# One streaming encoder layer on one core: the recurrence's two-operand GpSimd work goes to VectorE, and one PSUM bank goes from the projections to the recurrence

## The chip, the cores and the metric

The kernel runs on one core of a Trainium2 chip. The metric is the device time of one execution in microseconds, as the median of several runs. Every product is computed in float32 precision: a float32 operand is split into a high part (rounded to the matmul's input format) and a low part (the rest), and three matmuls (high x high, high x low, low x high) stand for one. So TensorE does three times the plain work, and each operand needs a cast on ScalarE and a subtraction on another engine.

## The reference

One layer of a hybrid encoder, 1024 prompt rows and 128 rows of running streams, model width 1024:

```
h = rms_norm(x); p = h @ w_in            # columns: RWKV r,k,v,loras | FoX q,k,v,forget | merge gates
u = p_r + (shifted(p_r) - p_r) * mu      # width-2 token shift
S_t = S_{t-1} * w_t + (S_{t-1} a_t) b_t + v_t k_t ;  y_t = S_t r_t     # 8 heads, 64 x 64 state
o_a = (groupnorm(y) + bonus) * g         # g = sigmoid(gate lora) @ g2: "the gate's product"
o_b = softmax(q k^T / 8 + c_t - c_s) v   # forgetting attention, 8 heads
x = x + (sig(g_a) * (o_a @ p_a) + sig(g_b) * (o_b @ p_b)) @ w_out
x = x + (silu(n @ w_gate) * (n @ w_up)) @ w_down ,  n = rms_norm(x);   y = rms_norm(x)
```

The decay w_t, a_t, b_t and k_t come from small lora products; kk, the normalised key, needs the sum of squares of a head's keys ("key sums").

## The kernel before, in words

The rows are normalised and transposed first. Then 14 column tiles of the RWKV projections run (`rwkv_tile`), and after them a long stretch in which TensorE alternates between the recurrence and more projections.

**The queue of projections.** `gemm_fm` cuts each projection tile (128 columns by 3 groups of 384 rows) into 8 pieces of 3 matmuls per group; the pieces stand in one list, `fq`. `D(n)` takes n pieces from it, `W(us)` takes as many as fill so many microseconds at 0.52 us each. Each group of rows of a tile accumulates in one PSUM bank of the pool `psg` (tag gm); the bank is free again when ScalarE and VectorE have read it (`evac`). The k and v tiles of the attention are transposed besides: a function `later`, put in `pending`, is run by `flush` behind the last matmul of the next tile, and its three transposes (L916) write a bank of the same pool. The weights of a tile are loaded one tile ahead (`w_in_tile`), cast by ScalarE (L146) and their low part subtracted (L147), on GpSimd for these tiles.

**The recurrence** (`rwkv_unit`) runs over 6 units of 192 rows (3 chunks of 64), all 8 heads at once. Per unit: products of the scaled keys and queries ("gram", L588), which are masked (`masked`, L581); the inverse of a triangular matrix, by a loop of 30 small VectorE operations (L617, L619) and products (L652 to L689); then three chunks in turn, each with a chain TensorE, VectorE, TensorE, VectorE and ScalarE, TensorE (L725, `solve_u`, L737, L748). The next unit's `prologue` (loras L438, key sums L447, bonus L497) and the previous unit's `epilogue` (mean L506, variance L512, gate's product L524) are generators that `step(nxt)` and `step(last)` move on by one stage, at written places in the unit. They, the gram, the transposes and the inverse take their PSUM banks from the pool `psr`, tag ms. Three more banks of `psr` hold the outputs y0, y1 and the chunk's products.

**The order.** In this stretch TensorE's order is the order in which the code is written (`manual_schedule`). The other engines' queues are ordered by a scheduler that goes by its own clock; `hi` asks it to put a step ahead, and instructions recorded through `hi` have the line of that helper, L388 in the kernel before (389 in the changed one). An engine works through its queue strictly in order.

Behind the recurrence come the attention of the prompt, one head after another, with the remaining projections between (`fox_d`), the streams' attention and the merge, the output product and the feed-forward part, which take the second half of the time.

Of the kernel before, what the change touches and what calls it, by code (L numbers as in the profile page):

```python
# [17 lines left out]
P = 128  # L18
# [35 lines left out]
def hybrid_kernel(ctx: ExitStack, tc: tile.TileContext, d, o):  # L54
# [110 lines left out]
    h_lo = [hp.tile([P, NK, G], F32R, name=f"hl{g}") for g in range(NG)]  # L165
    psg = pool("psg", 3, PSUM, side="right", stack=sth)
    stg = pool("stg", 2, side="right", stack=sth)
# [8 lines left out]

    def parameters(pl):
        prow = pl.tile([46, P], F32, name="prow", bufs=1)
# [9 lines left out]
        dma(sh_in, d["state_shift"][0, :, 0, :].rearrange("b (c p) -> (b c) p", p=P))  # L188
        pps = psg.tile([P, 512], F32, tag="gm", name="pps")
# [4 lines left out]
        shps = psg.tile([P, 512], F32, tag="gm", name="shps")  # L194
        T.transpose(shps[:, :14 * NB], sh_in, ident[:14 * NB, :14 * NB])
# [16 lines left out]
    def w_in_tile(c0, M):  # L212
        return load_w(wp1, d["w_in"][0, :, c0:c0 + M].rearrange("(k p) m -> p k m", p=P), NK, M, f"c{c0}", eng=GP)

# [73 lines left out]
    first += [rwkv_tile(ct) for ct in (4, 5)]  # L288
    with tc.tile_pool(name="ph0", bufs=3, reuse_waits="tile", side="left") as ph0:
        g1B = None  # L290
        for i in range(NTT):
            xt = ph0.tile([P, DM], F32, tag="xt", name="xt", bufs=6)
            dma(xt, xrow(i))
            if i == 0:
                g1B = row_gain(ph0, d["norm1_g"], "g1B")
            if i == 3:
                parameters(ph0)
            hn = ph0.tile([P, DM], F32, tag="hn", name="hn")
            norm_T(xt, hn, g1B, i, h_hi, h_lo, psg, "gm")
            if i % 3 == 2:  # L300
                for t_ in first:
                    fq += t_[NK * (i // 3):NK * (i // 3 + 1)]
            D(first_d[i])
        D(len(fq) - first_left)
        first.clear()
# [49 lines left out]
    def ms():  # L355
        return psr.tile([P, 512], F32, tag="ms", name="ms")

# [170 lines left out]
    def rwkv_unit(u_, us, nu, pre, last):  # L528
# [14 lines left out]
        V.tensor_tensor(BK[:, :, 2, :], ch3(k2), ch3(e3), op=mult)  # L543
        GP.tensor_tensor(BK[HS[1], :, 0, :], ch3(k2)[HS[1]], ch3(e3)[HS[1]], op=mult)

# [6 lines left out]
        for hd in range(2):  # L552
            GP.tensor_tensor(TT[HS[hd], :, hd, 1, :], ch3(ur)[HS[hd]], ch3(e2)[HS[hd]], op=mult)
        SV = [ch3(tt_()) for _ in range(2)]
# [17 lines left out]

        def masked(dst, src, c0, hs, eng=V):
            n0 = 0
            late_ = [final and (c0 + n) % NC3 >= 1 for n in range(4)]
            while n0 < 4:
                n1 = n0 + 1
                while n1 < 4 and late_[n1] == late_[n0]:
                    n1 += 1
                mk = (gmask_s if late_[n0] else gmask)[hs].unsqueeze(1).broadcast_to([hs.stop - hs.start, n1 - n0, 2, C])  # L580
                eng.tensor_tensor(dst[:, n0:n1], src[hs, n0:n1], mk, op=mult)  # L581
                n0 = n1

        for c0 in range(0, NC12, 4):
            pg = [psr.tile([P, 4, 2, C], F32, tag="ms", name="gram") for _ in range(2)]
            for c in range(4):
                for hd in range(2):
                    T.matmul(pg[hd][:, c], both(hd, c0 + c), TT[HS[hd], c0 + c, hd], start=True, stop=True)  # L588
            for hd in range(2):
                masked(GB[HS[hd], c0:c0 + 4], pg[hd], c0, HS[hd])  # L590
                S.copy(TT[OP[hd], c0:c0 + 4, hd], pg[hd][OP[hd]])
            W(2.1)
        step(last)
        for hd in range(2):
            for c0 in range(0, NC12, 4):
                masked(TT[OP[hd], c0:c0 + 4, hd], TT[:, c0:c0 + 4, hd], c0, OP[hd], GP)
        gab, grb = GB[:, :, 0, :], GB[:, :, 1, :]
# [7 lines left out]
        goff = tt_()[:, 0:NC12 * 32].rearrange("p (c t) -> p c t", t=32)  # L605
        GP.tensor_tensor(goff, dg[:, 0:NC12, :], low16.unsqueeze(1).broadcast_to([P, NC12, 32]), op=mult)
        L = inv_tile()
# [25 lines left out]
        V.transpose(XL[:, 0:32, :], X[:, 0:32, :])  # L633
        step(nxt)
        step(last)
        W(2.6)
        step(nxt)
        W(2.1)
        step(nxt)
        W(2.1)  # L640
        step(nxt)
        step(last)
        W(4.2)
        xd = XL[:, 0:32, 0:NC12].rearrange("p t c -> p c t")
# [75 lines left out]
        for c in range(ncp):  # L720
# [6 lines left out]
            for hd, hs in enumerate(HS):  # L727
                hi(GP.tensor_tensor, sts[hs], SV4[hd][hs, :, c, :], sc[hs, :, c:c + 1].broadcast_to([64, 4, 64]), op=mult)
            for y in range(4):
# [31 lines left out]
        def streams(z):  # L761
# [16 lines left out]
            for cc in range(2):  # L778
# [16 lines left out]
                for y in range(2):  # L795
                    i = (y0 + y) * NC3 + c
                    uvm = tt_()[:, 0:512].rearrange("p (h b t) -> p h b t", h=2, b=4)
                    Z = psr.tile([P, 512], F32, tag="ms", name="zs")[:, 0:256]
                    for hd, hs in enumerate(HS):
# [460 lines left out]
    def merge(g):  # L1260
        w, cur = [], []

        def piece(ct, q):
            if ct == 0 and q == 0:
                branch_b(g)
            if ct % 2 == 0 and q == 0:
# [4 lines left out]
                S.copy(hi, raw)  # L1271
                GP.tensor_tensor(lo, raw, hi.bitcast(F32), op=sub)
                w[:] = [hi, lo]
# [434 lines left out]
```

## Time and profile before

| | |
|---|---|
| runs | 2143.20, 2152.05, 2159.08 us; median 2152.05 |
| profiled execution | 2142.85 us, span 2141.1 us, granted clock 0.965 |
| busy, share of span | PE 1983.0 us (93%), VectorE 1213.8 (57%), ScalarE 822.5 (38%), GpSimd 358.7 (17%) |
| projections up to the recurrence | about 60 to 200 us: PE 140.0 of 140.0 us busy |
| recurrence, units 0 and 1 | 200 to 432 us: PE 205.2 us busy, clock 0.92 |
| recurrence, units 2 to 5 | 432 to 756 us: PE 298.9 us busy, clock 0.97 |
| streams of the recurrence, head 0 | 756 to 864 us: PE 94.3 us busy, clock 0.95 |

PE is TensorE, DVE VectorE, ACT ScalarE, POOL GpSimd. [...] A profile row is one of a stage table, a wait, a group of instructions, or one instruction in time; the times are us from the start of the span.

### The profile page before, as it was taken

How to read it: one execution, taken by the hardware profiler on the slowest of the kernel's cores; microseconds unless marked ns; L12 is line 12 of the kernel's file. 1: busy time of each engine (PE TensorE's matmuls, PEld its weight loads, DVE VectorE, ACT ScalarE, POOL GpSimd, SP SyncE). 2: the span in 40 equal slices, each digit the busy share in tenths (PEclk: the TensorE clock that was granted, in tenths of full speed). 3: DMA queues.
4: the chain of work that ended last, by engine and by line, in shares of the span. 5: the costliest groups of instructions: out<-in, count | busy, mean ns of one | idle time of the engine just before them, and what ended most of it. 6: DMA issues, size and time to landing. Idle time of an engine off the chain costs nothing. (4 is left out here: it accounts for less than half of the span.)

```text
span 2141.1 us, 38241 instructions
## 1 busy us (share of the span) xinstructions
PE 1983.0 (93%) x15472; PEld 1798.3 (84%) x15472; DVE 1213.8 (57%) x2274; ACT 822.5 (38%) x1569; POOL 358.7 (17%) x401
## 2 busy tenths in 40 slices
PE   7999988889898998879989898699999999999998
PEld 7998877778787977767868797699999999888887
DVE  5112576655756644668746524866666666564445
ACT  5323445362644433557644213522333223221113
POOL 3322423234243411010033103000000000000004
PEclk9999999899999999989999999799999999999999
DMA  5332333212221224676467517322312222452212
GB/s 168 108 92 87 106 91 95 66 57 73 64 62 49 81 73 107 175 208 178 129 209 249 160 58 247 97 78 71 95 62 73 71 67 89 143 208 84 84 63 89
DMA packets 234997, 233.66 MB, mean 109 GB/s; under 512 B 41678, under 2 KB 209252, under 8 KB 234820
## 3 DMA queue, kind: packets, MB, share of 16 engines
q1 hardware_dynamic: 163012, 159.85, 25.4%
q10 hardware_dynamic: 71280, 69.26, 9.7%
q8 instruction: 122, 2.00, 0.4%
q0 software_dynamic: 528, 2.10, 0.3%
q14 instruction: 55, 0.45, 0.1%
HBM read 157.53 MB, written 73.70 MB: 108 GB/s over the span
## 5 line engine op out<-in xcount | busy, mean ns | idle before, releaser
L152 PE MATMUL gm<-hh,hi_c 128*128 128x384 f32 (+1 forms) x1032 | 375.4, 364 | 1.5 <-DVE vl L928 0.7
L154 PE MATMUL gm<-hh,lo_c 128*128 128x384 f32 (+1 forms) x1032 | 353.0, 342 | 1.6 <-POOL lo_c L147 1.6
L153 PE MATMUL gm<-hl,hi_c 128*128 128x384 f32 (+1 forms) x1032 | 353.4, 342 | 0.3 <-DVE hl L136 0.3
L152 PEld LDWEIGHTS gm<-hh,hi_c 128*128 128x128 f32 (+1 forms) x1032 | 197.3, 191 | 17.6 <-issue 3.1
L153 PEld LDWEIGHTS gm<-hl,hi_c 128*128 128x128 f32 (+1 forms) x1032 | 197.4, 191 | 4.8 <-issue 0.8
L154 PEld LDWEIGHTS gm<-hh,lo_c 128*128 128x128 f32 (+1 forms) x1032 | 196.8, 191 | 4.4 <-POOL lo_c L147 2.2
L1619 PE MATMUL dn<-hi_d,ah 128*128 128x512 f32 x396 | 155.5, 393 | 4.0 <-ACT ah L1437 4.0
L1620 PE MATMUL dn<-lo_d,ah 128*128 128x512 f32 x396 | 155.0, 391 | 0.0
L1621 PE MATMUL dn<-hi_d,al 128*128 128x512 f32 x396 | 154.0, 391 | 0.0
L1639 POOL TENSOR_TENSOR yo<-x,gF 128x512 f32<-128x512 f32 x17 | 21.9, 1288 | 783.1 <-DVE x L1623 773.4
L147 POOL TENSOR_TENSOR lo_c<-raw_c,hi_c 128x1024 fp32r<-128x1024 f32 (+1 forms) x43 | 103.2, 2401 | 242.5 <-ACT hi_c L146 228.7
L1623 DVE TENSOR_TENSOR x<-x,dn 128x512 f32<-128x512 f32 x108 | 73.6, 686 | 114.5 <-PE dn L1621 113.7
L266 DVE SCALAR_TENSOR_TENSOR su<-gm,omu,sh 128x384 f32<-128x384 f32 (+1 forms) x42 | 24.1, 573 | 122.7 <-ACT sh L262 95.9
L1619 PEld LDWEIGHTS dn<-hi_d,ah 128*128 128x128 f32 x396 | 74.9, 189 | 20.5 <-ACT ah L1437 4.9
L1621 PEld LDWEIGHTS dn<-hi_d,al 128*128 128x128 f32 x396 | 74.9, 189 | 16.2 <-DVE al L1438 0.5
L1620 PEld LDWEIGHTS dn<-lo_d,ah 128*128 128x128 f32 x396 | 74.9, 189 | 15.5
L1437 ACT CAST ah<-raw_act 128x1152 fp32r<-128x1152 f32 x22 | 25.5, 1158 | 156.3 <-PE dn L1620 136.7
L1405 PE MATMUL po<-hi_o,mh 128*128 128x256 f32 x288 | 81.8, 285 | 4.0 <-ACT hi_o L146 4.0
L1406 PE MATMUL po<-lo_o,mh 128*128 128x256 f32 x288 | 82.0, 285 | 0.5 <-DVE lo_o L147 0.5
L1407 PE MATMUL po<-hi_o,ml 128*128 128x256 f32 x288 | 81.8, 284 | 0.0
L146 ACT CAST hi_c<-raw_c 128x1024 fp32r<-128x1024 f32 (+1 forms) x43 | 44.3, 1029 | 72.8 <-PE gm L153 62.0
L1508 PE MATMUL m<-t2h,s2h 128*128 128x256 f32 (+1 forms) x176 | 53.5, 304 | 12.3 <-ACT t2h L1437 12.3
(495 smaller groups left out, 5396.6 us busy)
## 6 DMA issues: line engine op xcount, KB each, us to landing
raw_c<-in_w_in SPq DMA_DIRECT2D x42, 512.0 KB
raw_act<-a_s SPq DMA_DIRECT2D x22, 576.0 KB
raw_w_gate<-in_w_gate SPq DMA_DIRECT2D x22, 512.0 KB
raw_w_up<-in_w_up SPq DMA_DIRECT2D x22, 512.0 KB
raw_d<-in_w_down SPq DMA_DIRECT2D x22, 512.0 KB
g_s<-sg ACTq DMA_DIRECT2D x48, 192.0 KB
u_s<-su ACTq DMA_DIRECT2D x42, 192.0 KB
a_s<-act ACTq DMA_DIRECT2D x22, 320.0 KB
```

The costliest lines, as they stand in the source:

```text
L147: eng.tensor_tensor(lo[:, :, c0:c0 + M], raw, hi[:, :, c0:c0 + M].bitcast(F32), op=sub)
L152: T.matmul(ps, wh(k), xh(k), start=(k == 0), stop=False)
L153: T.matmul(ps, wh(k), xl(k), start=False, stop=False)
L154: r = T.matmul(ps, wl(k), xh(k), start=False, stop=(k == nk - 1))
L1405: T.matmul(ps[:, :Q], mh, hi[:, k, :], start=(k == 0), stop=False)
L1406: T.matmul(ps[:, :Q], mh, lo[:, k, :], start=False, stop=False)
L1407: T.matmul(ps[:, :Q], ml, hi[:, k, :], start=False, stop=(k == NK - 1))
L1508: T.matmul(ps, ah[:, k, :], bh[:, k, :], start=(k == 0), stop=False)
L1619: T.matmul(ps, ah[:, ts_], wh[:, cs], start=(x == 0), stop=False)
L1620: T.matmul(ps, ah[:, ts_], wl[:, cs], start=False, stop=False)
L1621: T.matmul(ps, al[:, ts_], wh[:, cs], start=False, stop=(x == n - 1))
L1623: r = V.tensor_tensor(xs, xs, ps, op=add)
```

## The change

All two-operand GpSimd instructions of the recurrence and of the weights that run beside it become VectorE instructions: the low parts of the projection weights (L147) and of p_b (L1272), the key product BK (L544), two scalings TT (L553), the scaled state `sts`, the off-diagonal part `goff` (L606). The second half of the gram, which ScalarE copied out of PSUM (L591) and GpSimd then masked (L581), is masked by VectorE straight from PSUM; the ScalarE copy goes. The pool of the recurrence gets three banks for ms, that of the projections two; the normalisation before has its own four banks, freed before the recurrence begins. In the unit, the third stage of `last` (gate's product) stands ahead of the stage of `nxt` that has the key sums, its second stage gets a filler behind the first of `nxt`, and the fillers there are 26 pieces a unit, 24 before.

```diff
-    psg = pool("psg", 3, PSUM, side="right", stack=sth)
+    psg = pool("psg", 2, PSUM, side="right", stack=sth)
...
-        return load_w(wp1, d["w_in"][0, :, c0:c0 + M].rearrange("(k p) m -> p k m", p=P), NK, M, f"c{c0}", eng=GP)
+        return load_w(wp1, d["w_in"][0, :, c0:c0 + M].rearrange("(k p) m -> p k m", p=P), NK, M, f"c{c0}")
...
+            tc.tile_pool(name="ps0", bufs=4, reuse_waits="tile", space=PSUM, side="left") as ps0:
-            norm_T(xt, hn, g1B, i, h_hi, h_lo, psg, "gm")
+            norm_T(xt, hn, g1B, i, h_hi, h_lo, ps0, "gm")
...
     def ms():
-        return psr.tile([P, 512], F32, tag="ms", name="ms")
+        return psr.tile([P, 512], F32, tag="ms", name="ms", bufs=3)
...
-        GP.tensor_tensor(BK[HS[1], :, 0, :], ch3(k2)[HS[1]], ch3(e3)[HS[1]], op=mult)
+        V.tensor_tensor(BK[HS[1], :, 0, :], ch3(k2)[HS[1]], ch3(e3)[HS[1]], op=mult)
...
-            GP.tensor_tensor(TT[HS[hd], :, hd, 1, :], ch3(ur)[HS[hd]], ch3(e2)[HS[hd]], op=mult)
+            V.tensor_tensor(TT[HS[hd], :, hd, 1, :], ch3(ur)[HS[hd]], ch3(e2)[HS[hd]], op=mult)
...
                 masked(GB[HS[hd], c0:c0 + 4], pg[hd], c0, HS[hd])
-                S.copy(TT[OP[hd], c0:c0 + 4, hd], pg[hd][OP[hd]])
+                masked(TT[OP[hd], c0:c0 + 4, hd], pg[hd], c0, OP[hd])
             W(2.1)
         step(last)
-        for hd in range(2):
-            for c0 in range(0, NC12, 4):
-                masked(TT[OP[hd], c0:c0 + 4, hd], TT[:, c0:c0 + 4, hd], c0, OP[hd], GP)
...
-        GP.tensor_tensor(goff, dg[:, 0:NC12, :], low16.unsqueeze(1).broadcast_to([P, NC12, 32]), op=mult)
+        V.tensor_tensor(goff, dg[:, 0:NC12, :], low16.unsqueeze(1).broadcast_to([P, NC12, 32]), op=mult)
...
         step(nxt)
+        W(1.5)
         step(last)
-        W(2.6)
+        W(2.1)
         step(nxt)
         W(2.1)
         step(nxt)
         W(2.1)
+        step(last)
+        W(1.5)
         step(nxt)
-        step(last)
-        W(4.2)
+        W(2.6)
...
-                hi(GP.tensor_tensor, sts[hs], SV4[hd][hs, :, c, :], sc[hs, :, c:c + 1].broadcast_to([64, 4, 64]), op=mult)
+                hi(V.tensor_tensor, sts[hs], SV4[hd][hs, :, c, :], sc[hs, :, c:c + 1].broadcast_to([64, 4, 64]), op=mult)
...
-                GP.tensor_tensor(lo, raw, hi.bitcast(F32), op=sub)
+                V.tensor_tensor(lo, raw, hi.bitcast(F32), op=sub)
```

The order of VectorE's queue at the end of unit 1, before. `w_sb` and `t<-cp` are the two copies of the chunk's solve; TT belongs to the next unit.

```order
L388 TENSOR_TENSOR t_3253<-st_4173,sts_4133 64x4x64
L388 TENSOR_TENSOR t_3254<-st_4173,sts_4133 64x4x64
L388 COPY w_sb_4224<-cp_4204 128x256
L551 TENSOR_TENSOR TT_4277<-t_3635,t_3684 64x12x64 x2
L388 COPY t_3253<-cp_4204 64x4x64
L388 TENSOR_TENSOR st_4253<-cp_4204,sc_2763 128x256
L388 TENSOR_TENSOR st_4253<-st_4253,sts_4213 128x256
```

The same place in the changed kernel (one line number higher):

```order
L389 TENSOR_TENSOR t_3272<-st_4187,sts_4137 64x4x64
L389 TENSOR_TENSOR t_3273<-st_4187,sts_4137 64x4x64
L389 TENSOR_TENSOR sts_4217<-t_3272,sc_2767 64x256
L389 TENSOR_TENSOR sts_4217<-t_3273,sc_2767 64x256
L389 COPY w_sb_4228<-cp_4208 128x256
L552 TENSOR_TENSOR TT_4284<-t_3633,t_3692 64x12x64 x2
L389 COPY t_3272<-cp_4208 64x4x64
L554 TENSOR_TENSOR TT_4284<-u_3310,t_3798 64x12x64 x2
L389 TENSOR_TENSOR st_4260<-cp_4208,sc_2767 128x256
L389 TENSOR_TENSOR st_4260<-st_4260,sts_4217 128x256
```

The two `sts` now stand ahead of the first copy, the two TT of L552 stay ahead of the second copy, and the two TT that GpSimd had (L554 now) stand behind it.

VectorE's queue in unit 1 in the changed kernel, from the end of the epilogue's normalisation (L520) on: L457 is the scan of the next unit's decay, L526 the product that empties the banks of the gate's product.

```order
L520 TENSOR_TENSOR t_3025<-t_3025,t_2202 128x768
L457 SCALAR_TENSOR_TENSOR t_3798<-rmask_574,t_3692 128x768
L462 TENSOR_TENSOR t_3798<-t_3798,cm_3800 128x768
L526 TENSOR_TENSOR t_3025<-t_3025,ms_3747 128x384
L465 TENSOR_TENSOR t_3692<-t_3798,t_3692 128x768
L526 TENSOR_TENSOR t_3025<-t_3025,ms_3751 128x384
L147 TENSOR_TENSOR lo_c3592_3765<-raw_c3592_3762,hi_c3592_3764 128x1024
L486 TENSOR_SCALAR t_3813<-t_3691,prm_111,oka_113 128x192 x4
L487 TENSOR_TENSOR u_3306<-t_3813,u_3306 128x768
```

A weight's low part (L147) stands in this queue now. On TensorE the matmuls of the key sums (L448 in the changed kernel) follow those of the gate's product (L525) after nine matmuls of projections; before, the gate's product came right behind the key sums.

## Rows read from the trace of the kernel before

**Rows 1.** Stage table: stretch, length, busy us (instructions) by engine, TensorE clock, DMA, GB/s

```profile
200.00:432.00 232.00, 205.19 (x2118) 175.29 (x2118) 143.82 (x244) 103.49 (x193) 78.03 (x59) 0.92 0.30 87
432.00:756.00 324.00, 298.90 (x3571) 262.25 (x3570) 197.60 (x353) 160.82 (x275) 112.90 (x106) 0.97 0.21 63
```

**Rows 2.** Waits of PE: waiting tile and line, releaser: us in total, times, longest

```profile
PE ms L524 <- ACT t L448: 14.0, 4, 6.8
...
PE cp L737 <- ACT t L388: 10.9, 5, 3.5
...
PE pt L916 <- ACT sg L895: 8.7, 2, 4.7
...
PE ms L512 <- ACT t L628: 7.9, 3, 4.4
PE ms L438 <- ACT t L442: 6.2, 4, 2.1
PE lfps L860 <- DVE sg L854: 4.9, 1, 4.9
...
PE ms L660 <- ACT t L388: 3.9, 2, 3.7
```

**Rows 3.** Timeline, unit 2: start us, us, instruction, idle before it and releaser

```profile
466.15 2.50 POOL L147 TENSOR_TENSOR lo_c<-raw_c,hi_c 128x1024 fp32r<-128x1024 f32 x1 [1.11 <-ACT hi_c L146]
466.44 3.03 DVE L519 TENSOR_TENSOR t<-t 128x768 f32<-128x768 f32 x1
...
476.65 2.93 PE L524 MATMUL ms<-lo,lg 128*128 128x192 f32 x8 [6.84 <-ACT t L448]
```

**Rows 4.** Stage table of the four us behind that wait, columns as Rows 1

```profile
476.00:480.00 4.00, 3.35 (x10) 3.35 (x11) 0.56 (x2) 3.96 (x7) 0.00 (x0) 0.50 0.03 11
```

**Rows 5.** Timeline, end of unit 0

```profile
319.05 3.46 DVE L551 TENSOR_TENSOR TT<-t 64x768 f32<-64x768 f32 x2
319.09 5.08 POOL L553 TENSOR_TENSOR TT<-u,t 64x768 f32<-64x768 f32 x2 [0.60 <-PE yps L732]
...
322.54 0.42 DVE L388 COPY t<-cp 64x256 f32<-64x256 f32 x1
...
323.46 0.83 PE L737 MATMUL cp<-t 128*64 128x64 f32 x16 [1.86 <-ACT t L388]
```

**Rows 6.** One line's instructions: duration ns min/median/max, first and last start

```profile
L492 DVE SCALAR_TENSOR_TENSOR t<-u,prm x24: 404/406/2533, 215.9 to 664.1; 128x192 f32<-128x192 f32 x24
L551 DVE TENSOR_TENSOR TT<-t x12: 939/1711/2569, 226.2 to 689.7; 64x768 f32<-64x768 f32 x12
L1438 DVE TENSOR_TENSOR lo_d<-raw_d,hi_d x22: 1216/1222/1227, 1860.6 to 2085.8; 128x1024 fp32r<-128x1024 f32 x22
```

**Rows 7.** Groups in 200 to 835 us, POOL: busy us, mean ns, idle before

```profile
L147 POOL TENSOR_TENSOR lo_c<-raw_c,hi_c 128x1024 fp32r<-128x1024 f32 x26 | 63.1, 2426 | 121.1 <-ACT hi_c L146 118.6 <-issue 2.1 <-POOL sts L388 0.3
L581 POOL TENSOR_TENSOR TT<-TT,gmask 64x512 f32<-64x512 f32 x30 | 38.2, 1274 | 32.9 <-ACT TT L591 31.5
L553 POOL TENSOR_TENSOR TT<-u,t 64x768 f32<-64x768 f32 x12 | 30.1, 2508 | 11.9 <-ACT t L470 8.2 <-PE yps L732 3.3
```

**Rows 8.** The same stretch, DVE

```profile
L492 DVE SCALAR_TENSOR_TENSOR t<-u,prm 128x192 f32<-128x192 f32 x24 | 24.3, 1066 | 0.0
...
L581 DVE TENSOR_TENSOR GB<-gram,gmask 64x512 f32<-64x512 f32 x30 | 20.7, 688 | 43.9 <-PE gram L588 43.4
...
L388 DVE TENSOR_TENSOR t<-st,sts 64x256 f32<-64x256 f32 x20 | 8.6, 430 | 0.6
...
L905 DVE TENSOR_TENSOR lg<-gm,hg 128x384 fp32r<-128x384 f32 x6 | 3.3, 556 | 5.1 <-ACT hg L904 5.1
```

**Rows 9.** Timeline, unit 0: the transposes, and the evacuation of the tile before them

```profile
266.77 0.49 PE L916 MATMUL pt<-ident,sg 128*128 128x128 f32 x3
...
270.56 0.49 ACT L895 COPY sg<-gm 128x384 f32<-128x384 f32 x1
```

**Rows 10.** Groups in 200 to 835 us, ACT: a copy out of a projection bank

```profile
L895 ACT COPY sg<-gm 128x384 f32<-128x384 f32 x17 | 8.2, 480 | 3.1 <-PE gm L154 2.4 <-ACT vh L927 0.5
```

More of the change, by code (lines that the diff above doesn't have):

```diff
@@ L175, in hybrid_kernel, with parameters @@
     pcol = {}
-    def parameters(pl):
+    def parameters(pl, psp):
         prow = pl.tile([46, P], F32, name="prow", bufs=1)
@@ L188, in parameters @@
         dma(sh_in, d["state_shift"][0, :, 0, :].rearrange("b (c p) -> (b c) p", p=P))
-        pps = psg.tile([P, 512], F32, tag="gm", name="pps")
+        pps = psp.tile([P, 512], F32, tag="gm", name="pps")
         T.transpose(pps[:, :r0], prow[:r0, :], ident[:r0, :r0])
@@ L193, in parameters @@
         V.tensor_scalar(oka, prm[:, pcol["rwkv_k_a"]:pcol["rwkv_k_a"] + 4], -1.0, 1.0, op0=mult, op1=add)
-        shps = psg.tile([P, 512], F32, tag="gm", name="shps")
+        shps = psp.tile([P, 512], F32, tag="gm", name="shps")
         T.transpose(shps[:, :14 * NB], sh_in, ident[:14 * NB, :14 * NB])
@@ L288, in hybrid_kernel @@
     first += [rwkv_tile(ct) for ct in (4, 5)]
-    with tc.tile_pool(name="ph0", bufs=3, reuse_waits="tile", side="left") as ph0:
+    with tc.tile_pool(name="ph0", bufs=3, reuse_waits="tile", side="left") as ph0, \
+            tc.tile_pool(name="ps0", bufs=4, reuse_waits="tile", space=PSUM, side="left") as ps0:
         g1B = None
@@ L296, in hybrid_kernel @@
             if i == 3:
-                parameters(ph0)
+                parameters(ph0, ps0)
             hn = ph0.tile([P, DM], F32, tag="hn", name="hn")
-            norm_T(xt, hn, g1B, i, h_hi, h_lo, psg, "gm")
+            norm_T(xt, hn, g1B, i, h_hi, h_lo, ps0, "gm")
             if i % 3 == 2:
@@ L571, in rwkv_unit, with masked @@
         GB = rp.tile([P, NC12, 2, C], F32, tag="GB", name="GB", bufs=1)
-        def masked(dst, src, c0, hs, eng=V):
+        def masked(dst, src, c0, hs):
             n0 = 0
@@ L580, in masked @@
                 mk = (gmask_s if late_[n0] else gmask)[hs].unsqueeze(1).broadcast_to([hs.stop - hs.start, n1 - n0, 2, C])
-                eng.tensor_tensor(dst[:, n0:n1], src[hs, n0:n1], mk, op=mult)
+                V.tensor_tensor(dst[:, n0:n1], src[hs, n0:n1], mk, op=mult)
                 n0 = n1
         for c0 in range(0, NC12, 4):
-            pg = [psr.tile([P, 4, 2, C], F32, tag="ms", name="gram") for _ in range(2)]
+            pg = [psr.tile([P, 4, 2, C], F32, tag="ms", name="gram", bufs=3) for _ in range(2)]
             for c in range(4):
@@ L797, in streams @@
                     uvm = tt_()[:, 0:512].rearrange("p (h b t) -> p h b t", h=2, b=4)
-                    Z = psr.tile([P, 512], F32, tag="ms", name="zs")[:, 0:256]
+                    Z = psr.tile([P, 512], F32, tag="ms", name="zs", bufs=3)[:, 0:256]
                     for hd, hs in enumerate(HS):
```

## The prediction

> **What bounds the kernel now.** I read the stage table first. TensorE is the bound: in the 140 us before the recurrence it has no idle time. In the recurrence it loses time in two ways [rows 1]: from 200 to 756 us it is idle for 556 - 504.1 = 51.9 us, and its mean clock is 0.92 in units 0 and 1 and 0.97 in units 2 to 5, which is 0.08 x 232 + 0.03 x 324 = 28.3 us of a full clock. More than about 80 us can't be won there, whatever the other engines do; VectorE is busy for 62% and 61% of the two stretches.
>
> The list of TensorE's waits says what ends the idle time [rows 2]. Three entries are waits for a bank of the recurrence (tag ms), which ScalarE is late in emptying: the gate's product (L524) behind the key sums' logarithm, the variance (L512) behind the copies of the turned keys, the loras (L438) behind their own sigmoids, together 14.0 + 7.9 + 6.2 = 28.1 us in 11 waits. One is a wait for data, the chunk's last product (L737), 10.9 us in 5 waits, one at the end of each of units 0 to 4. The fifth entry (L916) is a transpose of the projections, after the recurrence.
>
> The timelines say why the releasers are late. At the end of unit 0 two VectorE products (L551) stand in the queue ahead of the copy that the chunk needs; they take 3.46 us while GpSimd works on two two-operand products of its own (L553), and TensorE waits 1.86 us [rows 5]. The same VectorE instruction takes 0.94 us at its shortest and 2.57 at its longest, another (L492) 0.404 and 2.533 [rows 6]: it stands still for about one GpSimd instruction, which take 1.3 to 2.5 us each [rows 7]. In unit 2 a VectorE addition (L519) takes 3.03 us beside a weight's subtraction on GpSimd, and the chain behind it in both queues ends in a wait of TensorE of 6.84 us [rows 3]. [...]
>
> **The change, part by part.**
>
> *Three banks for ms, and gate's product ahead of the key sums: -21 us.* Of the three, each waiter needs the bank that was given out two tiles earlier; now it is the one three tiles earlier, and before L512 and L524 there is more filler. What is new: the second key sum needs the bank of the gate's product, which VectorE empties only behind the scan of the next unit's decay. I take three quarters of 28.1 us as gone. Bounds: all of it, or half of it if the new wait is as long as each of the four it replaces.
>
> *The end of the unit: -9 us.* The two L551 stay ahead of the copy. Uncontended they take 2 x 0.94 = 1.9 us in place of 3.46, so 1.6 us of each of five waits goes, and more of the longest; about 0.3 us each is left: 10.9 - 1.5. The two scaled states that now stand ahead of the first copy take 2 x 0.43 [rows 8], while that copy waits for TensorE anyway. Bounds: 0 to -10.9.
>
> *The clock: -14 us.* These 16 waits of 39 us last 2.4 us on average, long enough for the low clock to follow. I take back half of 28.3 us, since units 0 and 1 get new waits (below). Bounds: 0 to -28.
>
> *VectorE's new work: 0.* It gets, over 200 to 835 us, 26 weights at 1.22 (by the same shape at L1438 [rows 6]) = 31.7, the second half of the masks at what the first half costs, 30 x 0.69 = 20.7 [rows 8] and some 6 for the shorter ones, 12 TT and 6 BK of 0.94 = 16.9, 32 states at 0.43 = 13.8, 6 small ones of about 0.55: 92 us. It is freed of standing still: for L492 24.3 - 24 x 0.404 = 14.6 [rows 6, 8]; for L551 the median alone is 0.77 above the shortest, 12 x 0.77 = 9.3; all VectorE groups of the stretch against their shortest instruction, 47 us. Net 45 us more in 635, so from 61% to about 68% busy. What hides it is that idle third. If the cover is gone, at most those 45 us come on top. ScalarE loses 36 copies, GpSimd nearly all it had; a cast or a fill that waited for those is not on TensorE's list.
>
> *Two banks for the projections: +22 us.* With two banks a group of rows starts in the bank of the group before the last; that is 24 matmuls back, some 4 us, and ScalarE's 0.5 us fits. Where a k or v tile is transposed it doesn't: the transpose takes one of the two banks, so the next group must wait for the group that has just ended. There are 24 such places, 12 in units 0 and 1, 12 near the end of the recurrence and in the first two heads. At the least such a wait is one evacuation: v one copy, 0.48 us; k copy, cast (taken as the copy) and subtraction, 0.48 + 0.48 + 0.56 = 1.5; q cast and subtraction, 1.05 [rows 8, 10]. Per column tile two k, three v, one q: 5.5 us, and with four column tiles 22 us. At the most: in unit 0 the evacuation began 3.8 us after the transpose, because ScalarE's queue waited for VectorE [rows 9]. Setting each evacuation's end in the trace against the start of the group that would need its bank gives 0.2 to 9.9 us in 26 places, a few of them without a transpose, 89 us together; the one shown ended 4.0 us late. I take the lower end, because what holds those evacuations up in the trace is VectorE standing still, and because units 0 and 1 wait already.
>
> *The rest: 0.* In the normalisation TensorE is held by its first row of work; p_b's subtractions release none of TensorE's larger waits [rows 2].
>
> The sum: -21 - 9 - 14 + 22 = -22 us on the profiled execution of 2142.85 us, 2121. That execution lies 0.43% under the median of the runs, 2152.05, so against the median I say **2130 us**.
>
> [...] The waits that took the clock down in the trace were of 1.8 us and more, and most of the 24 new ones are shorter, so I give them no clock. [...]
>
> **The rivals.**
>
> *The two banks cost their full price (slower).* Place: the 24 transposes. Price: 89 us of lateness, less the 17 of it that TensorE waits for already (L916 8.7, and in unit 0 4.9 at L860 and 3.7 at L660 [rows 2]), less 44 of gains: +28, so 2180 us. It decides where ScalarE's and VectorE's queues keep an evacuation behind the inverse's loop, as in [rows 9]; at 44 / 24 = 1.8 us a place the gain is gone, at 2.7 the kernel is slower by 1%. For it: those queues are in the same order as before at the transposes of unit 0. Against it: TensorE's wait lets the others catch up, so the lateness doesn't add up. [...]
>
> *The banks cost nothing more (more gain).* With VectorE never standing still, the evacuations come at once, and the 22 us lie in units 0 and 1 where TensorE would wait for VectorE's chain in any case. Then -44 to -60: 2092 to 2108 us.
>
> *VectorE becomes the bound of a unit.* Its 45 us net lie mostly in front of the solve, in one queue with the inverse. If half of it shows, the gain is gone: 2152 us. Against it: TensorE's waits in the trace name the inverse's products rarely. The same time would come if VectorE's long instructions had another cause than GpSimd and the change didn't do what it says.
>
> **How the numbers follow.** The forecast with its neighbours, 2116 to 2144, gets 0.50, of which 0.28 lie under 2130.5; the larger gain 0.17; VectorE as the bound 0.10; the full price of the banks 0.23, of which 0.20 over 2173.6. About 1% (21.5 us) is what a measurement of this kernel can tell from no change. So faster 0.28 + 0.17 = 0.45, within 1% 0.22 + 0.10 + 0.03 = 0.35, slower 0.20. The range reaches from the middle of the larger gain, 2097, up to 2172, short of the full price: a little under 2 in 10 is left outside.
>
> **What would show it.** The waits of L524, L512 and L438 nearly gone from TensorE's list, with a small new one at the key sums behind VectorE; L551 and L492 always at 0.94 and 0.40 us; waits for L737 under 0.5 us; a clock of 0.99 in units 2 to 5; new waits of 0.5 to 1.5 us at the first matmul of a projection group behind each L916, more in unit 0. It is wrong if these last waits are of 3 us and more and take the clock down, or if TensorE comes to wait for the inverse, or for a weight's low part behind VectorE.

## The result and the profile after

The changed kernel takes 2137.03 us (median of 16 runs, 2129.79 to 2146.76) against 2151.78 us of the kernel before (16 runs). The ratio is 0.9935, with a 95% interval of 0.992 to 0.9949: 15 us faster, where 22 had been forecast. The two profiled executions differ by less, 2141.1 and 2131.3 us of span, since that of the kernel before is one of its quicker ones; places are told below from the profiles, sizes of effects from the medians.

The stage table of the changed kernel, over the stretches of [rows 1]:

```profile
200.00:432.00 232.00, 205.14 (x2135) 174.36 (x2132) 157.34 (x291) 100.24 (x184) 5.57 (x12) 0.94 0.30 87
432.00:756.00 324.00, 305.40 (x3656) 272.06 (x3656) 226.07 (x437) 146.25 (x260) 11.59 (x25) 0.96 0.22 68
```

GpSimd is nearly empty now and VectorE 68% and 70% busy. But TensorE is as busy in the first stretch as before (205.14 against 205.19 us of 232) and gains 6.5 us in the next 324. Its clock is 0.94 and 0.96 where it was 0.92 and 0.97 (1.00 is full speed; both traces hold stretches at 1.00 and at 0.50 alone, and a value between is their mean over time). The two stretches are fixed and not the units themselves: unit 1 (up to the start of its last product, L737) ends at 427.4 us where it ended at 423.6 before, and units 2 to 5 take 320.7 us where they took 331.1. So in these two profiles the gain only begins with unit 2. TensorE's waits between 195 and 840 us are nearly as long together (56 us, 59 before), but they are others than those of [rows 2] (line numbers are the changed kernel's):

```profile
PE ms L660 <- ACT t L389: 17.4, 4, 5.4
PE gm L152 <- ACT sg L895: 10.7, 6, 2.7
PE gm L152 <- DVE vl L928: 6.7, 3, 3.4
PE cp L737 <- ACT t L389: 4.9, 5, 1.4
PE gm L152 <- DVE tg L918: 3.1, 4, 1.2
...
PE gm L152 <- DVE fx L861: 2.4, 3, 1.3
PE ms L440 <- ACT t L443: 2.1, 1, 2.1
```

The waits for an ms bank at the gate's product, the variance and the loras (28.1 us) are down to 2.9 us at L440, the 2.1 shown and one of 0.8. In their place stand waits for one of the two projection banks (L152, four lines, 22.9 us) and 17.4 us in which the inverse's second product (L660) waits for ScalarE's copy of the first. The prediction has a wait for the inverse only among the signs that would make it wrong.

The single instructions of [rows 6], and the weights' subtraction on its new engine:

```profile
L493 DVE SCALAR_TENSOR_TENSOR t<-u,prm x24: 408/415/415, 216.0 to 655.2; 128x192 f32<-128x192 f32 x24
L552 DVE TENSOR_TENSOR TT<-t x12: 940/953/956, 223.0 to 683.1; 64x768 f32<-64x768 f32 x12
L147 DVE TENSOR_TENSOR lo_c<-raw_c,hi_c x43: 226/1225/1228, 14.8 to 848.5; 128x1024 fp32r<-128x1024 f32 x42, 128x64 fp32r<-128x64 f32 x1
```

VectorE hardly stands still any more: the longest of the 24 L493 takes 0.415 us where it took 2.533. (At 826 us, beside the little that GpSimd still does, an L519 takes 1.17 us in place of 0.37.)

The new wait's cause is on the timeline of unit 2 (start us, us, engine, instruction):

```profile
476.03 1.28 ACT L449 ACT_TABLE_LOAD   x1 [0.39 <-ACT sg L942]
477.00 1.54 PE L652 MATMUL ms<-inv,t 32*32 32x32 f32 x96
477.32 1.05 ACT L449 ACTIVATE t<-ms,kkb 128x384 f32<-128x384 f32 x2
478.40 1.28 ACT L471 ACT_TABLE_LOAD   x1
479.69 0.84 ACT L471 ACTIVATE t<-t 128x768 f32<-128x768 f32 x1
480.44 0.83 ACT L450 ACTIVATE t<-t 128x768 f32<-128x768 f32 x1
...
481.39 1.28 ACT L942 ACT_TABLE_LOAD   x1
482.68 0.49 ACT L942 ACTIVATE sg<-gm 128x384 f32<-128x384 f32 x1
483.07 0.47 ACT L389 COPY t<-ms 128x384 f32<-128x384 f32 x1
...
483.59 0.60 PE L660 MATMUL ms<-inv,t 32*32 32x32 f32 x28 [3.79 <-ACT t L389]
```

The inverse's first product (L652) runs at 477.00. Its copy (the one L389 here) stands in ScalarE's queue behind the key sums' logarithm (L449) and exponential (L450), another exponential, a gate's sigmoid, and three table loads of 1.28 us, ahead of the logarithm, the first exponential and the sigmoid: it runs at 483.07, and L660 after 3.79 us of idle time.

So a part of what was won went into new waits. How much, and what had won it, the experiments show.

### The profile page after: what moved, and what is told of

It reads as the page before. It is cut to its first block, busy times and chain, and to the rows that moved or that the text cites. A ratio compares the mean times of both kernels' runs of the same rounds, so it can differ in the third digit from the quotient of the medians.

```text
span 2131.3 us, 38150 instructions
## 1 busy us (share of the span) xinstructions
PE 1982.1 (93%) x15472; PEld 1799.8 (84%) x15472; DVE 1269.0 (60%) x2433; ACT 799.4 (38%) x1531; POOL 106.3 (5%) x242
## 5 line engine op out<-in xcount | busy, mean ns | idle before, releaser
L152 PE MATMUL gm<-hh,hi_c 128*128 128x384 f32 (+1 forms) x1032 | 375.1, 364 | 24.9 <-ACT sg L895 10.7
L152 PEld LDWEIGHTS gm<-hh,hi_c 128*128 128x128 f32 (+1 forms) x1032 | 197.1, 191 | 45.5 <-ACT sg L895 12.5
L147 DVE TENSOR_TENSOR lo_c<-raw_c,hi_c 128x1024 fp32r<-128x1024 f32 (+1 forms) x43 | 51.6, 1200 | 75.7 <-ACT hi_c L146 75.4
L1621 PEld LDWEIGHTS dn<-hi_d,al 128*128 128x128 f32 x396 | 74.7, 189 | 16.8 <-DVE al L1438 1.1
L1083 PE MATMUL ptp<-ident,pp 128*128 128x128 f32 x288 | 53.5, 288 | 12.8 <-ACT pp L1071 10.3
L1532 ACT ACTIVATE act<-act 128x256 f32<-128x256 f32 (+1 forms) x88 | 39.2, 446 | 64.2 <-DVE act L1531 63.7
```

Of the source, the lines that this page charges most:

```text
L152: T.matmul(ps, wh(k), xh(k), start=(k == 0), stop=False)
L1083: T.transpose(ps[:, j * P:(j + 1) * P], pts[j][:, kt * P:(kt + 1) * P], ident)
L1621: T.matmul(ps, al[:, ts_], wh[:, cs], start=False, stop=(x == n - 1))
```

## The experiments

Every ratio is to the kernel before, run beside it on the same chip, with its 95% interval. The parts of the change were first put in one after another.

**The moves to VectorE alone** (also the masks straight from PSUM; three banks for projections, two for ms, steps as before):

```diff
 # against the changed kernel
-    psg = pool("psg", 2, PSUM, side="right", stack=sth)
+    psg = pool("psg", 3, PSUM, side="right", stack=sth)
...
-        return psr.tile([P, 512], F32, tag="ms", name="ms", bufs=3)
+        return psr.tile([P, 512], F32, tag="ms", name="ms")
...
-        W(1.5)                    # the steps of nxt and last as in the kernel before
...
```

> The kernel before with only the move of GpSimd's two-operand work to VectorE and the masks straight from PSUM; banks stay 3 for projections and 2 for ms, the steps of the next unit stay in the old order. Theory (the gain is shared: both the moves and the third ms bank give, the two projection banks take): the waits at the chunk's last product fall from 10.9 to about 5 us, VectorE's L492 is always at 0.41 us, the two-bank waits of TensorE (24 us in the changed kernel) are not there, the waits for an ms bank stay near 28 us: 2140 us, ratio 0.995. Rival A (the moves alone are the gain, the banks only cost): 2120 us or less, ratio 0.985. Rival B (VectorE's 45 us of new work take back what the missing contention gives): 2152 us, ratio 1.000.

Measured: 2109.61 us, 0.981 (0.9792 to 0.9827). That is 41 us, rival A: the moves are more than the whole gain, and the rest of the change costs 27. My own theory of a shared gain falls. Its stage table, for units 0 and 1 and for units 2 to 5 (which end at 400.9 and 723.8 us, in the kernel before at 423.6 and 754.7):

```profile
200.00:400.90 200.90, 189.27 (x2080) 161.61 (x2078) 150.41 (x281) 93.00 (x174) 6.57 (x13) 0.98 0.33 97
400.90:723.80 322.90, 303.54 (x3595) 265.88 (x3594) 228.80 (x442) 149.06 (x259) 11.57 (x25) 0.97 0.22 66
```

The kernel before does the same units in this way:

```profile
200.00:423.60 223.60, 196.79 (x2064) 168.69 (x2063) 141.10 (x238) 100.15 (x183) 76.14 (x57) 0.93 0.30 88
423.60:754.70 331.10, 306.00 (x3592) 267.72 (x3592) 199.87 (x357) 162.88 (x282) 114.67 (x108) 0.96 0.21 64
```

In units 0 and 1 TensorE's idle time falls from 26.8 to 11.6 us, and what the clock takes (one minus the clock, times the length) from 15.7 to 4.0. The waits at the chunk's last product are down from 10.9 to 1.8 us; the ms waits at the gate's product are not (12.1 of 14.0):

```profile
PE ms L524 <- ACT t L448: 12.1, 4, 5.8
...
PE cp L734 <- ACT t L388: 1.8, 4, 1.0
```

**Two projection banks besides, one bank left empty:**

```diff
 # against the moves alone
-    psg = pool("psg", 3, PSUM, side="right", stack=sth)
+    psg = pool("psg", 2, PSUM, side="right", stack=sth)
...
```

The normalisation gets its own four banks with it, as in the change; the recurrence begins at 199 to 200 us with and without them.

> The moves to VectorE, the old order, two banks for the projections and only two for ms (one bank stays empty): the price of the two projection banks alone. Theory (prices add up: +24 us in units 0 and 1, +4 in the first heads, which the third ms bank then gave back in part): 2110 + 28 = 2138 us, ratio 0.993. Rival (a wait for a projection bank hides a wait for an ms bank, so that the price was partly the third bank's own): 2120 us, ratio 0.985.

Measured: 2135.3 us, 0.9921 (0.9895 to 0.9946), as the theory had it: the two banks cost 26 us. It is all there by the end of unit 1, which comes at 427.3 us in place of 400.9:

```profile
200.00:427.30 227.30, 198.30 (x2071) 168.77 (x2071) 151.41 (x281) 95.02 (x175) 5.31 (x11) 0.94 0.29 85
```

Idle time is 29.0 us (11.6 with three banks) and the clock takes 13.6 (4.0). The waits are those for the last reader of a k or v tile's bank:

```profile
PE gm L152 <- ACT sg L893: 10.8, 7, 3.4
PE gm L152 <- DVE vl L926: 8.7, 2, 5.0
```

In units 0 and 1 there are 14 waits for a projection bank, 24.0 us in all. The clock falls to 0.50 at six waits of 2.5 to 5.0 us (five of these 14, and one of 4.0 us at the gate's product), and it stays at 1.00 at the other nine waits for a bank, of up to 1.5 us.

**The third ms bank besides** (the changed kernel with the steps in the old order):

```diff
 # against the changed kernel
         step(nxt)
-        W(1.5)
         step(last)
-        W(2.1)
+        W(2.6)
         step(nxt)
         W(2.1)
         step(nxt)
         W(2.1)
-        step(last)
-        W(1.5)
         step(nxt)
-        W(2.6)
+        step(last)
+        W(4.2)
```

> The changed kernel with the next unit's and the last unit's steps in the old order and old filler (key sums ahead of the gate's product, 4.2 us of filler behind both). Theory: the copy of the inverse's first product is late in the changed kernel because the key sums' logarithm and exponential and their table loads now stand right ahead of it in ScalarE's queue; with the old order the 17.4 us of waits at the inverse's second product fall to under 5, of the old wait at the gate's product (14.0 us with two banks) some 4 come back: 2128 us, ratio to before 0.989. Rival (the reorder is a part of the gain, the late copy would be late in any order): the wait at the gate's product comes back whole and the other stays: 2147 us, ratio 0.998.

Measured: 2118.14 us, 0.9846 (0.9829 to 0.9862), 10 us less than the theory had. Against the run before, the third bank gives 17 us; against the changed kernel, the new order of the steps with its filler costs 19. The wait at the inverse's second product (L658 here) is 4.0 us in place of 17.4, and the gate's product (L525 here) waits 7.1 us, where it waits 14.2 with two ms banks:

```profile
PE ms L658 <- ACT t L389: 4.0, 2, 3.7
...
PE ms L525 <- ACT t L449: 3.7, 2, 3.0
PE ms L525 <- DVE t L526: 3.4, 2, 2.7
```

Along this path the steps are -41.1 for the moves, +25.7 for the two banks, -17.2 for the third ms bank and +18.9 for the order, together -13.7 where the change, in its own runs, measures -14.8. Steps along one path add up whatever they are; that they don't depend on one another is another question.

**The banks alone,** with GpSimd's work left where it was, ask the same from the other side:

```diff
 # against the kernel before
-    psg = pool("psg", 3, PSUM, side="right", stack=sth)
+    psg = pool("psg", 2, PSUM, side="right", stack=sth)
...
-        return psr.tile([P, 512], F32, tag="ms", name="ms")
+        return psr.tile([P, 512], F32, tag="ms", name="ms", bufs=3)
...
```

> The kernel before with only the banks changed: 2 for projections, 3 for ms, a pool of its own for the normalisation; GpSimd keeps its two-operand work, steps in the old order. Theory: some 21 of the 28 us of ms waits go, 24 us of two-bank waits come, more where VectorE stands still beside GpSimd: 2155 us, ratio 1.002. Rival A (the banks only cost): 2167 us or more, ratio 1.007. Rival B (the banks are the gain): 2137 us, ratio 0.993.

Measured: 2159.25 us, 1.0037 (1.0024 to 1.0051): a loss of 8.6 us, between the theory and rival A. With the moves the same trade of banks costs 8.5 us, and so the moves give 41 us with either division of the banks (2159.25 to 2118.14, and 2150.68 to 2109.61): these two parts hardly depend on one another.

**Why do the moves give 41 us?** Two accounts were open: VectorE no longer stands still beside GpSimd, or the chains over two queues became shorter. First, useless GpSimd products beside the moves: VectorE does all the real work, and GpSimd multiplies the same inputs into a part of a tile that nobody reads.

```diff
 # against the moves alone; likewise beside BK, the masks (GB times GB) and the states
             V.tensor_tensor(TT[HS[hd], :, hd, 1, :], ch3(ur)[HS[hd]], ch3(e2)[HS[hd]], op=mult)
+            GP.tensor_tensor(junk, ch3(ur)[HS[0]], ch3(e2)[HS[0]], op=mult)
```

> The moves alone, and beside them GpSimd works on 86 two-operand products whose results nobody reads, in places like those from which the work was moved (18 of 64x768, 36 of 64x512, 32 of 64x256; about 107 us in all). VectorE does all of the real work. Theory (VectorE standing still beside GpSimd's two-operand work is the cause, whoever needs the result): more than half of the 31 us is lost again, 2128 us, ratio 0.990, with VectorE's L492 back at up to 2.5 us. Rival (the gain came from the shorter chains, the work being on one engine's queue): 2111 us, ratio 0.981, since nobody waits for the new products.

Measured: 2143.75 us, 0.9957 (0.994 to 0.9973): 34 of the 41 us are lost again, more than the theory had, by work of which nothing waits for the result (between 195 and 840 us no wait of another engine ends on GpSimd). The timeline at the end of unit 2 shows how:

```profile
501.60 1.88 POOL L546 TENSOR_TENSOR BK<-u,t 64x768 f32<-64x768 f32 x1
...
501.82 2.48 DVE L542 SCALAR_TENSOR_TENSOR BK<-t 128x768 f32<-128x768 f32 x1
...
503.56 4.87 POOL L556 TENSOR_TENSOR BK<-u,t 64x768 f32<-64x768 f32 x2
...
504.22 2.55 DVE L543 TENSOR_TENSOR BK<-u,t 128x768 f32<-128x768 f32 x1
506.70 0.41 DVE L388 COPY w_sb<-cp 128x256 f32<-128x256 f32 x1
507.14 2.11 DVE L544 TENSOR_TENSOR BK<-u,t 64x768 f32<-64x768 f32 x1
507.16 1.12 PE L718 MATMUL cp<-w_sb,t 64*64 64x64 f32 x16 [4.15 <-DVE w_sb L388]
```

Beside GpSimd's products those of VectorE, of 0.95 us in the moves alone, take 2.11 to 2.55, and the copy behind them in its queue is late for TensorE by 4.15 us; five such waits make 18.9 us. One thing differs besides: in the moves alone VectorE's queue has the BK products ahead of the chunks, and here right ahead of that copy. At 0.95 us each they would have held it up there too, by 1.9 us in place of 5.0; the other 3.1 us are the standing still. So it is in three of the five waits; of the other two one has a single BK product ahead of the copy, and one a BK product and a weight's low part. The new place in the queue is thus a part of the 34 us; the next run is free of it.

**The weights back on GpSimd:**

```diff
 # against the moves alone
-        return load_w(..., f"c{c0}")
+        return load_w(..., f"c{c0}", eng=GP)
```

> The moves alone (3 and 2 banks, old order; 2110 us), but the low parts of w_in's weights go back to GpSimd, 26 of them of 2.4 us in the recurrence. Theory (VectorE standing still beside GpSimd is what the moves took away, and a GpSimd instruction costs by its length): the weights were 63 of 191 us of GpSimd's work in the recurrence, so a third of the 31 us that the moves gave there goes: 2120 us, ratio 0.986. Rival A (they fall on VectorE at any time, the inverse too, and are the worst): 2128 us or more, ratio 0.990. Rival B (VectorE is spared 32 us of its own work, which makes good for it): 2110 us, ratio 0.981.

Measured: 2126.11 us, 0.9877 (0.9855 to 0.9899): 16 us lost, between theory and rival A. VectorE has 26 x 1.22 us less to do in the recurrence and yet the kernel is slower; L492 reaches 2.5 us again:

```profile
L492 DVE SCALAR_TENSOR_TENSOR t<-u,prm x24: 405/410/2528, 215.1 to 644.5; 128x192 f32<-128x192 f32 x24
```

**The masks back on ScalarE and GpSimd:**

```diff
 # against the moves alone
-                masked(TT[OP[hd], c0:c0 + 4, hd], pg[hd], c0, OP[hd])
+                S.copy(TT[OP[hd], c0:c0 + 4, hd], pg[hd][OP[hd]])
...
+                masked(TT[OP[hd], c0:c0 + 4, hd], TT[:, c0:c0 + 4, hd], c0, OP[hd], GP)
```

> The moves alone, but the second half of the masks goes the old way: ScalarE copies it out of PSUM (36 copies) and GpSimd masks it in place (48 us). Theory (the cost is VectorE standing still, by GpSimd's length): a quarter of the 31 us goes, 2118 us, ratio 0.985. Rival A (the chain over ScalarE and GpSimd held the chunk's first product): 2125 us or more, ratio 0.988. Rival B (the cover is deep there): 2110 us, ratio 0.981.

Measured: 2107.85 us, 0.9799 (0.9774 to 0.9824), not to be told from the moves alone. The theory that a GpSimd instruction costs by its length fails here: 48 us of GpSimd products, and nothing lost. VectorE's part of the same line keeps its length beside them:

```profile
L581 DVE TENSOR_TENSOR GB<-gram,gmask x38: 272/684/695, 238.7 to 681.7; 64x512 f32<-64x512 f32 x30, 64x128 f32<-64x128 f32 x8
L581 POOL TENSOR_TENSOR TT<-TT,gmask x38: 448/1272/1295, 240.1 to 684.3; 64x512 f32<-64x512 f32 x30, 64x128 f32<-64x128 f32 x8
```

On the timeline these GpSimd masks lie beside nothing of VectorE's for some 35 of their 48 us, and of the rest all but 1 us beside VectorE instructions that read an operand from PSUM, its own masks above all (8 of the 30 wide ones). What counts is not GpSimd's work but how long VectorE stands still for it. Worked out from the groups of VectorE between 200 us and the end of the first head's preparations (number times mean, less the same number times the mean in the moves alone):

| kernel | VectorE stands still, us | time over the moves alone, us |
|---|---|---|
| kernel before | 45.0 | 41 |
| useless products | 32.2 | 34 |
| weights back | 22.2 | 16 |
| masks back | 1.8 | -2 |

Between 0.7 and 1.1 us of time for each us of standing still, in a queue that was idle for a third of the stretch.

**Why does the order cost 19 us?** First the copy of the inverse's first product on the other engine:

```diff
 # against the changed kernel
-        hi(S.copy, p0, ps[:, :NB32])
+        hi(V.tensor_copy, p0, ps[:, :NB32])
```

> The changed kernel with the one copy of the inverse's first product on VectorE in place of ScalarE. Theory: it no longer stands behind two table loads and a gate's sigmoid; in VectorE's queue it stands behind one product that waits for the key sums' exponential, so each of the 4 waits of 4.4 us shrinks by about 2: 8 us in all, 2129 us, ratio 0.989. Rival (what ends the wait is the unit's chain in whatever queue; the time is lost again at the next product): 2137 us, ratio 0.993.

Measured: 2134.9 us, 0.9917 (0.9901 to 0.9934), not clearly better than the changed kernel, as the rival had it. The waits of the second product are 14.9 us in place of 17.4: in VectorE's queue the copy stands behind a product (L452) that needs the key sums' exponential, so the late chain holds it there too.

For a cleaner look the banks were given out in another way. **A bank of the transposes' own:** two banks for the projections' groups and one for their transposes, ms keeps two.

```diff
 # against the moves alone
-    psg = pool("psg", 3, PSUM, side="right", stack=sth)
+    psg = pool("psg", 2, PSUM, side="right", stack=sth)
+    pst = pool("pst", 1, PSUM, side="right", stack=sth)
...
-                pt = psg.tile([P, 3, P], F32, tag="gm", name="pt")
+                pt = pst.tile([P, 3, P], F32, tag="pt", name="pt")
...
```

> As the run with the shared bank, but the third bank belongs to the transposes of the projections throughout and ms has two banks throughout. Theory: of the 26 us between the moves alone (2110) and the shared bank (2084) 18 are the third ms bank of units 2 to 5 and 8 the transposes' own bank: 2102 us, ratio 0.977. Rival (all of it is the third ms bank): 2110 us, ratio 0.981.

Measured: 2105.61 us, 0.9777 (0.975 to 0.9804): 4 us better than the moves alone by the medians, 7 by the ratios, with intervals that overlap, so the theory's 8 us are neither shown nor excluded. **The same bank shared** with ms from unit 2 on, where few transposes run:

```diff
 # against the own bank
     def ms(shape=(P, 512), name="ms"):
         turn[0] += 1
         if deep and turn[0] % 3 == 0:
             return pst.tile(list(shape), F32, tag="pt", name=name)
         return psr.tile(list(shape), F32, tag="ms", name=name)
...
+            if u_ >= 2:
+                deep.append(u_)
```

> The moves to VectorE and the old order of the steps, and a bank of its own for the turned tiles of the projections: 2 banks for the projections' groups, 1 for the transposes, 2 for ms in units 0 and 1; from unit 2 on ms takes its every third tile from the bank of the transposes. Theory: the third ms bank is worth 18 us in units 2 to 5 (between the two runs with the moves alone and with moves and banks), the two projection banks cost 24 in units 0 and 1 and 4 in the first heads, and this kernel has the one without the other: 2110 - 18 = 2092 us, ratio 0.973. Rival: the transposes and the recurrence get in each other's way on the shared bank at the end of the recurrence, or the third bank's gain was only the time by which the projections were late: 2110 us, ratio 0.981.

Measured: 2083.84 us, 0.9681 (0.9661 to 0.9701). It is the fastest of all, 8 us faster than the theory had and 53 us faster than the changed kernel by the medians. It has the third ms bank (22 us more than with the transposes' own) without the price of the two projection banks.

On this kernel **only the two steps were swapped**, filler and place as before:

```diff
 # against the shared bank
-        step(nxt)
         step(last)
+        step(nxt)
         W(4.2)
```

> The shared bank with only the gate's product put ahead of the key sums, both at the place of the old order, filler as before: key sums don't come later, the gate's product comes one step earlier. Theory (the swap itself is good, what cost was that the key sums came later): the 9.3 us in which the gate's product waits for the key sums' logarithm go, TensorE's clock follows: 2076 us, ratio 0.965. Rival (the wait moves to the key sums, whose bank VectorE empties late, or to the inverse's first product): 2084 us or a little more, ratio 0.968.

Measured: 2090.94 us, 0.9713 (0.9689 to 0.9737): 7 us slower than without the swap, the rival. The wait at the gate's product (9.3 us in 3 places) is gone, and in its place the inverse's second product (L665 here) waits 12.4 us in 5 places, 10.2 more than before, and the key sums 3.4. Unit 2 in the kernel with the shared bank (of the timeline the key sums' logarithm L456, the gate's product L532, the inverse's products L657 and L665 and the copy L396):

```profile
446.51 1.05 ACT L456 ACTIVATE t<-ms,kkb 128x384 f32<-128x384 f32 x2
447.14 1.65 PE L532 MATMUL ms<-lo,lg 128*128 128x192 f32 x4 [5.52 <-ACT t L456]
...
454.06 1.54 PE L657 MATMUL ms<-inv,t 32*32 32x32 f32 x96
455.67 0.48 ACT L396 COPY t<-ms 128x384 f32<-128x384 f32 x1 [1.44 <-PE ms L657]
456.79 0.93 PE L665 MATMUL ms<-inv,t 32*32 32x32 f32 x52
```

and in the one with the swap, with what ScalarE does between:

```profile
449.32 1.05 ACT L456 ACTIVATE t<-ms,kkb 128x384 f32<-128x384 f32 x2
450.39 1.28 ACT L947 ACT_TABLE_LOAD   x1
451.27 1.54 PE L657 MATMUL ms<-inv,t 32*32 32x32 f32 x96
451.68 0.49 ACT L947 ACTIVATE sg<-gm 128x384 f32<-128x384 f32 x1
...
456.67 0.47 ACT L396 COPY t<-ms 128x384 f32<-128x384 f32 x1
457.20 1.00 PE L665 MATMUL ms<-inv,t 32*32 32x32 f32 x56 [3.12 <-ACT t L396]
```

TensorE, spared its wait, comes to the inverse 2.8 us earlier, though unit 2 began 2.4 us later here (first gram at 409.7 and 407.3 us). ScalarE does not: from the decay's cumulated sum on, its queue is filled almost without a gap by exponentials, the logarithm, gates' sigmoids and their table loads, and the copy behind them runs at 456.67. The wait at the gate's product was for the most part the place where TensorE waited for this chain; without it TensorE waits at the next products that need the two engines. In unit 2 that comes out even or a little better (waits of 5.6 us in place of 5.5, and a unit 1.5 us shorter); the loss lies in units 1 and 3, where the gate's product had waited for 0 and 0.7 us and L665 now waits for 2.9 and 2.7. By the profiles units 0 to 5 lose 3.8 us of the 6.3 in all; where the others are lost, behind the recurrence, stays open.

**The whole new order on the shared bank:**

```diff
 # against the shared bank: the steps and filler of the changed kernel
         step(nxt)
+        W(1.5)
         step(last)
...
+        step(last)
+        W(1.5)
         step(nxt)
-        step(last)
-        W(4.2)
+        W(2.6)
```

> The shared bank with the steps as the change orders them (gate's product, 1.5 us of filler, key sums, 2.6 us of filler, inverse). Theory (key sums that late put their logarithm, exponential and table loads right ahead of the copy of the inverse's first product, with any banks): the wait of 4 us in units 1 to 4 is there again, and 13 to 16 us are lost: 2099 us, ratio 0.975. Rival (the order only cost because it met the projections' two banks): 2084 us or less, ratio 0.968.

Measured: 2111.44 us, 0.9808 (0.9782 to 0.9834): 28 us lost, more than the theory's 13 to 16. The expected wait is there, in five places, and one of 8.1 us for a projection bank:

```profile
PE ms L667 <- ACT t L396: 18.8, 5, 5.1
PE gm L152 <- DVE lg L908: 8.1, 1, 8.1
```

So the order costs with either division of the banks. Not all of it is told by that wait: the new order also takes 12 more pieces of the projections into the recurrence, about 6 us at 0.52 each, and the swap alone costs 7. From 200 us to the end of the recurrence the changed kernel takes 604.8 us and the old order 588.0, on the shared bank 587.4 and 564.8. Of the 16.8 us 7.0 are idle time of TensorE and 9.8 busy time, of the 22.6 us 12.9 and 9.7. In the busy time are the 6 us of the 12 pieces and a lower clock (0.95 and 0.97, 0.96 and 0.98). The pieces taken early should be saved later, but they aren't: behind the recurrence the new order takes 1327 us where the old one takes 1328, and 1324 against 1318 on the shared bank, where the wait of 8.1 us stands (it ends at 826 us, behind the recurrence). Why so little is saved there stays open.

## Why the prediction was right, and where it was not

The forecast of 2130 lay 7 us under the time, and its reasons are another matter: two large terms of it were wrong, in opposite directions, and that they nearly cancelled is luck.

*VectorE's new work: 0.* This is the step that failed, by size. It set 47 us of standing still that go against 92 us of new work and called both hidden by VectorE's idle third. The net work is hidden indeed, as VectorE is 70% busy and no wait names a weight's low part. But standing still isn't spread like work: it falls on whatever is next in the queue, in the run with the useless products at five places a copy out of PSUM for which TensorE waited, 18.9 us together. All in all the moves are worth 41 us, where the forecast had 9 at the end of the units and a part of the clock. The prediction's own 47 us were near the right size, had the excess of each VectorE group been priced as time.

*The end of the unit: -9.* In the moves alone the waits at the chunk's last product fall by 9.1 us, as forecast. In the changed kernel 4.9 us are left, three times the forecast, and with the old order 1.8: the order's doing.

*Three ms banks and gate's product ahead: -21.* Two edits in one term. The third bank alone measures -17, near the forecast for both; the new order, gate's product ahead and filler, measures +19, so the term as a whole is +2. I had named the key sums behind VectorE as what would be late next, and that wait is small: 3.4 us in the kernel with the swap. What is late next is on ScalarE, whose queue I had read only as the releaser of the old wait. That L448 took long to come was on its timeline, with the table loads ahead of it; I took it for a shortage of banks.

*Two projection banks: +22.* Measured 26, and the full price of 89 us didn't come. But the 22 were added up from 24 short waits of 0.5 to 1.5 us, half of them near the end of the recurrence or later. In the run with two and two banks all of the 26 us is there by the end of unit 1: its 14 waits take 24.0 us, the longest 4.96, and the clock falls; the places behind the recurrence cost nothing that shows in the time. So the size of a wait was too small and the number of places that count too large, and that the total is near is luck again. In the changed kernel the four lines of 10.7, 6.7, 3.1 and 2.4 us are 16 waits, the longest of 3.4 us, which is in part the sign of being wrong that the prediction had named.

The clock was given nothing for these banks. With nothing but the bank taken away, that of units 0 and 1 goes from 0.98 to 0.94, which is 9.6 us. There the clock fell at the long waits, of 2.5 to 5.0 us, and at none of the nine short waits for a bank, of up to 1.5 us. So giving short waits no clock was borne out; the waits that came were longer. The 1.8 us that the prediction set as the least wait that takes the clock down in the trace of before is not quite right: it fell there at 398.95 us too, behind a wait of 1.33 us (L680).

*The clock: -14.* Of the 16 waits that were counted as long enough, the profile before has the clock fall to 0.50 at ten, of 1.75 to 6.84 us (behind the longest as in [rows 4]), and not at the other six, of 0.20 to 2.11. With the moves alone the clock is 0.98 in units 0 and 1, and 11.7 us come back there. The changed kernel gives that away to its new waits: over the two stretches of [rows 1] 0.94 and 0.96 make 26.9 us of a full clock, where they were 28.3; in units 2 to 5 0.99 had been expected.

*What should show it.* L493 and L552 (L492 and L551 before) came as forecast, and the gate's product and the variance are off the list. A wait for the inverse was named as what would make it wrong, and it came. VectorE as the bound of a unit is out: with the shared bank it does the same work 53 us sooner.

## What to carry to other kernels

Price a contended engine by how much longer its instructions take than they take undisturbed, group by group; here that excess, and not its busy share, was the time to be won, 0.7 to 1.1 us for each of its us in the three runs where it showed. Before removing a wait by moving work, follow the queue of its releaser: if that queue is full up to the next thing TensorE needs, the wait only moves, as 9.3 us at the gate's product became 12.4 at the inverse here. And a resource that two stages need at different times (a PSUM bank here) can be handed over between them, which was worth more than either fixed split (2083.84 us against 2109.61 and 2118.14).

## What the runs showed of the hardware

In the run with the useless products VectorE's products with both operands in SBUF stood still beside GpSimd's and its masks with one operand in PSUM didn't. Of the former, three at the end of unit 2 take 2.11 to 2.55 us in place of 0.95, while all 30 wide masks of the second half, which read PSUM, lie beside GpSimd's products and take 0.696 us at most (0.695 in the changed kernel, where GpSimd has no such products):

```profile
L584 DVE TENSOR_TENSOR TT<-gram,gmask x38: 273/683/696, 245.7 to 715.7; 64x512 f32<-64x512 f32 x30, 64x128 f32<-64x128 f32 x8
```

So masks straight from PSUM were safe on VectorE beside these products. But two operands in SBUF aren't the only case: with the weights back on GpSimd, four `tensor_scalar` (L518, which reads one tile and columns of scalars) of 0.37 us each take 3.17 together, the first of them 2.30, beside a weight's low part:

```profile
625.60 2.34 POOL L147 TENSOR_TENSOR lo_c<-raw_c,hi_c 128x1024 fp32r<-128x1024 f32 x1
...
625.76 3.17 DVE L518 TENSOR_SCALAR t<-t,prm 128x192 f32<-128x192 f32 x4
```

Why L518 is held up where the masks are not, no run shows.

ScalarE's changes of function fill its queue where logarithm, exponential and sigmoid alternate. In the changed kernel there are five table loads of 1.28 us between the scan's copy (470.63 us) and the copy that the inverse waits for (483.07): 6.4 of 12.4 us.
